# Outgoing products of the first feed-forward block: seven half-size products in place of eight, in three groups

## The chip, the cores and the metric

The kernel runs on one core of one Trainium2 chip. It runs one layer of an encoder on 512 tokens of width 1024, in 32-bit floats. The metric is the time of one execution on the device in microseconds, median of several runs. A core has five engines that work side by side, each through its own queue in order: TensorE (PE in the profile) multiplies, VectorE (DVE) and ScalarE (ACT) do elementwise work, GpSimd (POOL) and SyncE (SP) mostly issue transfers here. Transfers are carried out by 16 DMA engines.

## The reference

The layer has three parts. The first and the third are feed-forward blocks (SwiGLU), the second mixes tokens by two kinds of attention. The change is in the first block:

```python
h = modulate(rmsnorm(x, norm_ffn1[l]), sh1, sc1)
x = x + 0.5 * g1[:, None, :] * swiglu(h, w_ffn1_in[l], w_ffn1_out[l])
# swiglu(h, w_in, w_out): gate, up = split(h @ w_in); (silu(gate) * up) @ w_out
# mod = silu(c) @ w_mod + b_mod gives sh1, sc1, g1 and six more vectors (9 x 1024)
```

x is 512 x 1024, the inner width is 2816. In the kernel everything lies transposed: x is eight tiles (128 rows of the width by 512 tokens), and the inner width is 22 chunks of 128. An outgoing product takes one chunk of activations (128 x 512 tokens) and a 128 x 128 piece of w_ffn1_out, for each of eight output columns m.

## The kernel before

**High and low parts.** [...] To keep precision each operand is split into a high part (an ACT cast, L185) and a low part (a DVE subtraction, L186; `split_from`), and each product is done three times: high by high, high by low, low by high (`mm3`, L174 to L176, for 512 tokens or 256; `two`, L444 to L446, for 256).

**Seven for eight.** A `Unit` multiplies a 2 x 2 matrix of half-size blocks by another with seven products in place of eight (Strassen's way, in Winograd's form). Its seven products are called s1, a11, a12, s2, s3, s4, a22. Three of the weight operands come from HBM by plain loads and the others are made by adding: `ask` loads a block (SP), adds another to it in flight for s1 (`accum_op=ALU.add`, issued by POOL), and `prepare` splits the block into high and low parts and then has POOL add the next block to what lies in the buffer, for the next operand. The result is put together from copies of PSUM banks (ACT, L521) and sums (DVE, L523, L528, L531, after a12, s4 and s3). Operands on the side of the activations are sums as well (`SUMS`): n1, n2, t3, t4 beside b11, b12, b21, b22, of which seven are used.

**First block.** Of the 22 chunks of the inner width the first six are computed by plain products (the first three of them right at the start, beside the norm), and the others in pairs, p = 3 to 10, by eight units of depth 4 (`in_unit1`), at seven for eight. What they leave (`finish`, `in_post1`) is split into high and low parts and kept. The outgoing products are plain (`Out1`): `CHUNKS` has four groups of chunks (0 to 5, 6 to 11, 12 to 15, 16 to 21), and after the units that yield a group's chunks, each of the eight output columns m is multiplied and added to x by DVE (L802, with the gate g1). The last group ends in `boundary`, which does its last `LAST_1` = 4 columns first for tokens 0 to 255 and then for 256 to 511, with the next norm's sums, diagonal and spread at given steps (`TO_MIX`).

**Last block.** It does both its ingoing and its outgoing products by units: after each group of pairs (`PARTS`: 4, 4 and 3) follow two outgoing units, one for each half of the width.

**What sets the order.** `run_items` goes through a list of products. A product's loads are asked for a few products ahead (`ASK`, counted in products of full length) and its weights are split a few ahead (`MAKE`). SP and POOL work strictly in the order in which this list issues; PE, DVE and ACT are put in order by the framework's scheduler. Five places for high and low weight parts (`HILO`) and four for raw weights (`RAW`) are shared. Beside the products the list spends a credit of 0.27 for each (`SIDE`): each full credit lets one of 24 remaining columns of w_mod (512 KB) be loaded by SP and reduced by DVE (`mod_col`, L272). These are needed for g1 (the gate of the outgoing products) and for the next norm.

Of the kernel before, what the change touches and what calls it, by code (L numbers as in the profile page):

```python
# [18 lines left out]
P = 128  # L19
D = 1024  # L20
T = 512
# [87 lines left out]
CHUNKS = (range(0, 6), range(6, 12), range(12, 16), range(16, 22))  # L109
PLAIN, LAST_1 = 3, 4  # L110
# [24 lines left out]
def layer(ctx: ExitStack, tc: tile.TileContext, a: dict):  # L135
# [434 lines left out]

    def sub(out, p, q, negated):

        if negated:
            V.scalar_tensor_tensor(out, p, -1.0, q, ALU.mult, ALU.subtract)
        else:
            V.tensor_tensor(out, p, q, ALU.subtract)
# [26 lines left out]
    cact = [sbuf("ka", [P, D], F32, 1)]  # L603
    hh, hl = new_h()
# [111 lines left out]
    act1 = {}  # L716

    def act_of(p):
        if p not in act1:
            act1[p] = b8()  # L720
        return act1[p]
# [14 lines left out]
    def in_post1(c, v, u):  # L736
# [12 lines left out]
        t, r = act_of(u.p), HALVES[int(c[2]) - 1]  # L749
        split_from(t[:, 0:2, r], t[:, 2:4, r], g.rearrange("p (j q) -> p j q", j=2))  # L750
# [7 lines left out]
    class Out1:  # L758


        def __init__(self, chunks, tag, final):
            self.chunks, self.tag, self.final, self.depth = chunks, tag, final, len(chunks)
            self.length = len(chunks) / 4
            self.ASK, self.MAKE = {m: 3.0 for m in range(NC)}, {m: 1.5 for m in range(NC)}
            self.at, self.ready, self.bank = {}, {}, {}

        def ask(self, m):
            if m not in self.at:
                n, c = self.depth * P, self.chunks.start * P
                t = self.at[m] = sbuf("raw", [P, 1024], F32, RAW)[:, 0:n]  # L770
                nc.sync.dma_start(t, a["w1o"][m][:, c : c + n])

        def by_halves(self, m):
            return self.final and m >= NC - LAST_1

        def prepare(self, m):
            if m not in self.ready:
                self.ask(m)
                aside = FAR if not self.by_halves(m) else STEP_1 if m == NC - LAST_1 else ASIDE
                t = self.ready[m] = high_low(self.depth * P, aside, (self, m))  # L780
# [3 lines left out]
        def products(self, m, po, r, ks):  # L784
            wh, wl = self.ready[m]
            for k in ks:
                q, o = self.chunks[k], slice(k * P, (k + 1) * P)
                t = act_of(q // 2)
                mm3(po, wh[:, o], wl[:, o], t[:, q % 2, r], t[:, 2 + q % 2, r], k == 0, k == self.depth - 1)
                if k == self.depth - 1 and r.stop == T:  # L790
                    let_go((self, m))
                yield

        def multiply(self, m, ks=None):
            if m not in self.bank:
                self.bank[m] = bank(self.tag)
            list(self.products(m, self.bank[m], FULL[0], range(self.depth) if ks is None else ks))

        def after(self, m):
            while any((v, c) == (G1, m) for v, c, *_ in rest + asked):  # L800
                column(rest)
            V.scalar_tensor_tensor(x[m], self.bank[m], modv[G1][:, m : m + 1], x[m], ALU.mult, ALU.add)  # L802
            if self.final:
                n2.add(m)
                spill(m)
# [3 lines left out]
    def item1(u, q, ks=None):  # L809
        items1.append((u, q, ks, side1))  # L810
# [24 lines left out]
    with tc.manual_schedule(engines={mybir.EngineType.SP, mybir.EngineType.Pool}):  # L835
# [4 lines left out]
        for q in range(3, 2 * PLAIN):  # L840
# [12 lines left out]
            finish(q, out)  # L853
            if q == 3:
# [4 lines left out]
        begun = PLAIN  # L859
        for n, chunks in enumerate(CHUNKS):  # L860


            final = n + 1 == len(CHUNKS)
            for p in range(begun, max(chunks.stop // 2, PLAIN + 1)):
                u, nxt = units1[p], units1.get(p + 1)
                if p == PLAIN:
                    item1(u, "s1")
                    item1(u, "a11")
                elif p > begun:
                    item1(units1[p - 1], "a22")  # L870
                if p == PLAIN or p > begun:
                    item1(u, "a12")
                item1(u, "s2")
                if nxt:
                    item1(nxt, "s1")
                item1(u, "s3")
                item1(u, "s4")
# [1059 lines left out]
```

## Time and profile before

| what | before |
|---|---|
| median of 3 runs | 1066.88 us (1066.68 to 1067.96) |
| profiled execution, span | 1066.6 us |
| instructions | 18660 |
| moved by DMA | 220.92 MB |

The profile is of one execution. Its page gives each engine's busy time, then the span in 40 slices (26.7 us each) with a digit for the busy tenths, the DMA queues with the time that their packets took as a share of all 16 engines over the span, and groups of instructions: line, engine, operation, output and inputs, shapes, count, busy time, mean of one in ns, idle time before them and what ended it. A view by windows gives the same sums for given stretches. PE's busy time counts products; PEld counts the weight loads that run beside them. A "share" of DMA is the time that packets took, over 16 engines.

### The profile page before, as it was taken

The page shows a single profiled execution, that of the slowest core. Times are in us where ns is not written, and L with a number is a line of the kernel's source. Part 1 is how long each engine was busy: PE and PEld are TensorE (multiplying, and loading weights), DVE is VectorE, ACT ScalarE, POOL GpSimd, SP SyncE. Part 2 cuts the span into 40 slices and gives each one's busy share as a digit, 9 for nine tenths or more (in the row PEclk, how much of TensorE's full clock was granted, in tenths as well). Part 3 has the DMA queues.
Part 4 walks back from the last instruction along what each step waited for, and adds up shares of the span by engine and source line. Part 5 has one row for each costly group of instructions (what it writes and reads, how often), then busy time and mean ns, then how long its engine had stood idle before and what let it go on. Part 6 is the DMA issues. An engine that isn't in the chain of part 4 may idle for free.

```text
span 1066.6 us, 18660 instructions
## 1 busy us (share of the span) xinstructions
PE 1047.0 (98%) x7316; PEld 953.3 (89%) x7316; DVE 795.7 (75%) x1459; ACT 566.6 (53%) x928; POOL 155.0 (15%) x174
## 2 busy tenths in 40 slices
PE   7999999999999999999999999999999999999998
PEld 5689889899899998888777878989999999999997
DVE  6985666666796679858864578976889777877867
ACT  5564334344354342667676755534766646654553
POOL 1100010100110100443211100001011211112210
PEclk9999999999999999999999999999999999999999
DMA  9968687866975459696356852974498998999974
GB/s 332 362 205 208 207 211 189 264 155 195 281 181 160 164 200 409 215 270 160 99 120 166 239 160 85 351 242 118 101 232 200 215 230 217 220 219 213 219 146 124
DMA packets 69084, 220.92 MB, mean 207 GB/s; under 512 B 8194, under 2 KB 10882, under 8 KB 68995
## 3 DMA queue, kind: packets, MB, share of 16 engines
q1 hardware_dynamic: 46512, 146.52, 38.2%
q0 software_dynamic: 19488, 68.70, 34.9%
q10 hardware_dynamic: 2994, 4.51, 1.2%
q8 instruction: 57, 0.93, 0.3%
q14 instruction: 33, 0.26, 0.1%
HBM read 209.46 MB, written 10.23 MB: 206 GB/s over the span
## 4 chain that ended last, share of the span: by engine, by line
PE 79%; DVE 8%; issue 5%; DMA 3%; ACT 3%; POOL 1%; SPq 0%; ACTq 0%; DVEq 0%; POOLq 0%
PE acc L444 5%; PE acc L446 5%; PE acc L445 5%; PE sc L174 5%; PE sc L175 5%; PE sc L176 5%; PE sc L446 5%; PE sc L444 5%; PE sc L445 5%; PE acc L174 4%; PE acc L176 4%; PE acc L175 4%; PE sc L182 2%; PE acc L1048 2%; PE acc L1049 2%
## 5 line engine op out<-in xcount | busy, mean ns | idle before, releaser
L185 ACT CAST high<-raw 128x1024 fp32r<-128x1024 f32 (+2 forms) x162 | 158.3, 986 | 165.9 <-PE acc L445 38.8
L186 DVE TENSOR_TENSOR low<-raw,high 128x1024 fp32r<-128x1024 f32 (+2 forms) x162 | 183.7, 1141 | 61.2 <-ACT high L185 60.2
L444 PE MATMUL acc<-b,high 128*128 128x256 f32 x508 | 141.0, 278 | 0.3 <-DVE f L523 0.3
L446 PE MATMUL acc<-b,low 128*128 128x256 f32 x508 | 140.6, 277 | 0.2 <-DVE low L186 0.2
L445 PE MATMUL acc<-b,high 128*128 128x256 f32 x508 | 140.6, 277 | 0.1
L444 PE MATMUL sc<-b,high 128*128 128x256 f32 x500 | 138.5, 277 | 1.8 <-ACT f L521 1.8
L446 PE MATMUL sc<-b,low 128*128 128x256 f32 x500 | 138.6, 277 | 1.1 <-DVE low L186 1.1
L445 PE MATMUL sc<-b,high 128*128 128x256 f32 x500 | 138.4, 277 | 0.0
L186 DVE TENSOR_TENSOR low<-u,high 128x1024 fp32r<-128x1024 f32 (+1 forms) x73 | 87.5, 1200 | 28.4 <-ACT high L185 27.1
L185 ACT CAST high<-u 128x1024 fp32r<-128x1024 f32 (+1 forms) x73 | 75.5, 1035 | 56.5 <-PE sc L175 15.9
L174 PE MATMUL sc<-b,high 128*128 128x512 f32 (+1 forms) x280 | 100.8, 360 | 0.0
L175 PE MATMUL sc<-b,high 128*128 128x512 f32 (+1 forms) x280 | 100.4, 359 | 0.0
L176 PE MATMUL sc<-b,low 128*128 128x512 f32 (+1 forms) x280 | 100.2, 358 | 0.0
L444 PEld LDWEIGHTS acc<-b,high 128*128 128x128 f32 x508 | 95.4, 188 | 0.8 <-DVE f L523 0.5
L444 PEld LDWEIGHTS sc<-b,high 128*128 128x128 f32 x500 | 94.0, 188 | 2.2 <-ACT f L521 2.2
L445 PEld LDWEIGHTS acc<-b,high 128*128 128x128 f32 x508 | 95.5, 188 | 0.4 <-DVE b L1725 0.3
L446 PEld LDWEIGHTS acc<-b,low 128*128 128x128 f32 x508 | 95.4, 188 | 0.4 <-DVE low L186 0.4
L446 PEld LDWEIGHTS sc<-b,low 128*128 128x128 f32 x500 | 93.9, 188 | 1.5 <-DVE low L186 1.5
L445 PEld LDWEIGHTS sc<-b,high 128*128 128x128 f32 x500 | 93.9, 188 | 0.0
L174 PE MATMUL acc<-b,high 128*128 128x512 f32 (+1 forms) x248 | 92.7, 374 | 0.0
L176 PE MATMUL acc<-b,low 128*128 128x512 f32 (+1 forms) x248 | 90.0, 363 | 0.0
L175 PE MATMUL acc<-b,high 128*128 128x512 f32 (+1 forms) x248 | 89.8, 362 | 0.0
(369 smaller groups left out, 2676.4 us busy)
## 6 DMA issues: line engine op xcount, KB each, us to landing
u<-w_mod SPq DMA_DIRECT2D x40, 512.0 KB, 7.6
b<-w_mod SPq DMA_DIRECT2D x32, 512.0 KB, 6.0
raw<-w2i SPq DMA_DIRECT2D x31, 512.0 KB, 5.9
u<-w2i POOLq DMA_DIRECT2D x31, 512.0 KB, 6.6
u<-w1u POOLq DMA_DIRECT2D x24, 512.0 KB, 7.1
raw<-w1u SPq DMA_DIRECT2D x24, 512.0 KB, 6.8
raw<-w1o SPq DMA_DIRECT2D x24, 384.0 KB, 4.5
raw<-w_gate SPq DMA_DIRECT2D x16, 512.0 KB, 6.8
```

Source lines behind the costliest of these rows:

```text
L174: PE.matmul(out, wh, xh, start=first, stop=False)
L175: PE.matmul(out, wh, xl, start=False, stop=False)
L176: PE.matmul(out, wl, xh, start=False, stop=last)
L182: PE.matmul(out, of[j][a], of[j][b], start=i == 0, stop=i == 2)
L185: S.copy(hi, src)
L186: V.tensor_tensor(lo, src, f(hi), ALU.subtract)
L444: PE.matmul(out, wh[:, s], xh, start=first and j == 0, stop=False, skip_group_check=True)
L445: PE.matmul(out, wh[:, s], xl, start=False, stop=False, skip_group_check=True)
L446: PE.matmul(out, wl[:, s], xh, start=False, stop=last and j == 1, skip_group_check=True)
L1048: PE.matmul(out[t][:, 0:n], hh[k][:, ht], wh[:, o : o + n], start=k == 0, stop=False)
L1049: PE.matmul(out[t][:, 0:n], hh[k][:, ht], wl[:, o : o + n], start=False, stop=False)
```

## The change

Of the 22 inner chunks, the first 18 (pairs 0 to 8, `PARTS_1`: three groups of three pairs) now go out through units of depth 3: two after each group (`out_unit1`), one for each half of the width. Only the last four chunks (pairs 9 and 10) go out plainly (`Last1`), and `LAST_1` becomes 6, so that six of eight columns are done by halves of the tokens in `boundary`.

For that the activations of pairs 0 to 8 are no longer split whole. `late1` hands each pair to `act_split`, which makes the four differences and splits seven operands of 256 tokens; these come in pieces, one or two beside each product. They are kept in four of the big tiles (`act_tile`), in a new tile `extra` (tag "tabs", whose place the rotary tables take later, in place of `keep` tiles of their own) and in halves of the first block's h that are no longer read (`slot`). The differences of sign that the units need are put into a negated copy of the gate (`minus`). Weights are laid out anew (`w1a`, `w1o`).

```diff
-CHUNKS = (range(0, 6), range(6, 12), range(12, 16), range(16, 22))
-PLAIN, LAST_1 = 3, 4
+PARTS_1 = (range(0, 3), range(3, 6), range(6, 9))
+PLAIN, LAST_1 = 3, 6
...
+    def act_split(b, store):
+        ta, tb = f2(), f2()
+        b.update(n1=ta[:, T1], n2=ta[:, T2], t3=tb[:, T1], t4=tb[:, T2])
+        for o in ("n1", "b11", "b21", "n2", "b22", "t3", "t4"):
+            if o in SUMS:
+                sub(b[o], *(b[q] for q in SUMS[o]), o in NEGATED)
+            hi, lo = store(o)
+            split_from(hi, lo, b[o])
+            yield
...
     def finish(q, out):
-        s, m = f2(), f2()
-        S.activation(s, out[0], AF.Silu)
-        V.tensor_tensor(m, s, out[1], ALU.mult)
-        t = act_of(q // 2)
-        split_from(t[:, q % 2, :], t[:, 2 + q % 2, :], m)
+        values1[q] = m = f2()
+        S.activation(m, out[0], AF.Silu)
+        V.tensor_tensor(m, m, out[1], ALU.mult)
...
+    def out_unit1(part, g):
+        def post(c, v, u):
+            n, t = int(c[1]) - 1, int(c[2]) - 1
+            for j in range(2):
+                m = 4 * g + 2 * n + j
+                xr = x[m][:, HALVES[t]]
+                by = gate_column(m)
+                V.scalar_tensor_tensor(xr, v[:, j * H : (j + 1) * H], by, xr, ALU.mult, ALU.add)
+
+        r = slice(part.start * 2 * P, part.stop * 2 * P)
+        srcs = {q: a["w1a"][g, i][:, r] for i, q in enumerate(("a11", "a12", "a21", "a22"))}
+        u = Unit(srcs, len(part), lambda o, k: act1[o, part.start + k], post, 0)
+        u.p, u.in_order, u.length = None, ("s2", "s4"), len(part) / 4
+        return u
...
+        seq = [units1[PLAIN]]
+        for part in PARTS_1:
+            seq += [units1[p] for p in range(max(part.start, PLAIN) + 1, part.stop + 1) if part.start]
+            seq += [out_unit1(part, g) for g in range(2)]
+        seq += [units1[p] for p in range(PARTS_1[-1].stop + 1, NH)]
...
+        out = Last1()
+        for m in range(2):
+            item1(out, m, ks=range(2), rest=True)
+        for m in range(2):
+            item1(out, m, ks=range(2, out.depth))
+        for m in range(2, NC - LAST_1):
+            item1(out, m)
```

So the order of the first block becomes: unit 3, two out units (pairs 0 to 2), units 4 to 6, two out units (pairs 3 to 5), units 7 to 9, two out units (pairs 6 to 8), unit 10, the plain stage with four chunks.

More of the change, by code (lines that the diff above doesn't have):

```diff
@@ L955, in layer @@
         else:
-            C, R = (keep([P, NT, HD], f"{n}{nm}") for n in "CR")
+            C, R = (four(tabs)[2 * (nm == "kb") + i] for i in range(2))
         g0 = row[:, o : o + NF].unsqueeze(1).broadcast_to([P, NT, NF])
@@ L1813, in late @@
             act_begin()
-        steps = act_split(units[p], p - part.start)
+        u = units[p]
+        b = {f"b{n + 1}{t + 1}": u.v[f"g{t + 1}"][:, r] for t in range(2) for n, r in enumerate(HALVES)}
+        steps = act_split(b, act_store(p - part.start))
         pending.extend([lambda: next(steps)] * 7)
```

212 lines of the change are left out of this document (134 added, 78 removed).

## The prediction

> **What bounds the kernel now.** The page first: busy times, and the slices of the span.
>
> ```profile
> PE 1047.0 (98%) x7316; PEld 953.3 (89%) x7316; DVE 795.7 (75%) x1459; ACT 566.6 (53%) x928; POOL 155.0 (15%) x174
> PE   7999999999999999999999999999999999999998
> DVE  6985666666796679858864578976889777877867
> PEclk9999999999999999999999999999999999999999
> DMA  9968687866975459696356852974498998999974
> q1 hardware_dynamic: 46512, 146.52, 38.2%
> q0 software_dynamic: 19488, 68.70, 34.9%
> ```
>
> PE is busy for 1047.0 of 1066.6 us, at the full granted clock in every slice. So a product removed shortens the run, as long as the others keep up; what they have left decides. The first block's stages came next. These are its inner units and plain outgoing stages in turn: unit 3, out, units 4 and 5, out, units 6 and 7, out, units 8 to 10. Columns: length, then busy time of PE, PEld, DVE, ACT and POOL, granted clock, DMA share, GB/s.
>
> ```profile
> 89.96:117.39 27.43, 27.43 (x241) 27.42 (x240) 19.52 (x27) 13.98 (x20) 0.86 (x1) 1.00 0.60 169
> 117.39:150.06 32.67, 32.67 (x147) 27.03 (x145) 20.15 (x28) 7.97 (x9) 3.46 (x4) 1.00 0.80 225
> 150.06:190.52 40.46, 38.68 (x338) 38.48 (x336) 28.63 (x38) 20.31 (x27) 3.45 (x4) 1.00 0.75 208
> 190.52:223.18 32.66, 32.66 (x146) 27.03 (x145) 17.99 (x26) 7.97 (x9) 3.48 (x4) 1.00 0.91 269
> 223.18:262.85 39.67, 38.91 (x338) 38.53 (x336) 28.72 (x37) 20.30 (x28) 3.45 (x4) 1.00 0.57 146
> 262.85:284.63 21.78, 21.78 (x98) 18.02 (x97) 16.18 (x22) 7.26 (x10) 2.59 (x3) 1.00 1.00 291
> 284.63:334.16 49.53, 49.53 (x434) 49.33 (x432) 41.04 (x72) 26.83 (x37) 5.80 (x7) 1.00 0.74 194
> ```
>
> From 89.96 to 334.16 us, 244.2 us, PE idles 2.5 us (1.78 in the third row, 0.76 in the fifth). DVE's busy times add up to 172.2 us (0.71 of the stretch). The DMA shares times the lengths give 183.7 us (0.75). Both have room, most of it in the plain outgoing stages, where DVE is busy for 0.55 to 0.74 of the time. Those stages are what the change takes away.
>
> The last block already does its outgoing products in the new way. Three windows of it:
>
> ```profile
> 780.00:825.00 45.00, 45.00 (x397) 45.00 (x396) 39.76 (x65) 30.26 (x49) 7.82 (x9) 1.00 0.93 213
> 853.00:900.00 47.00, 47.00 (x414) 47.00 (x414) 36.04 (x52) 24.34 (x34) 7.87 (x10) 1.00 0.96 236
> 970.00:1000.00 30.00, 30.00 (x266) 30.00 (x265) 22.95 (x36) 13.74 (x21) 4.88 (x6) 1.00 0.95 227
> ```
>
> There PE does not idle with DVE at 0.77 to 0.88 and the DMA engines at 0.93 to 0.96. But that block has no w_mod columns beside it; the first block has 24.
>
> **The change, part by part.**
>
> *PE.* Removed: 18 chunks x 8 columns of output x 3 = 432 products 512 wide. An outgoing stage is 6 x 8 x 3 = 144 of them in 32.67 us: 0.2269 us each, 98.0 us. Added: 6 out units x 7 x 18 = 756 products 256 wide. The 853 window has 414 of these in 47.00 us: 0.1135 us each, 85.8 us. PE gains 12.2 us. The last four chunks stay plain: six columns by halves with four chunks are 24 steps of 0.34 us, as four columns with six chunks were, so the passage to the mixers keeps its length and I cost it at nothing. What hides the norm's chain there is the nine steps between its sums (step 4) and its spread (step 13), 3.1 us; without that cover PE would wait about as long.
>
> [...]
>
> *DVE.* Rows of the first and last block (count, busy us, mean ns of one), and two neighbours of the timeline:
>
> ```profile
> L186 DVE TENSOR_TENSOR low<-raw,high 128x768 fp32r<-128x768 f32 x24 | 22.6, 952 | 10.2 <-ACT high L185 10.2
> L186 DVE TENSOR_TENSOR low<-u,high 128x1024 fp32r<-128x1024 f32 x21 | 25.7, 1223 | 5.3 <-ACT high L185 4.8
> L802 DVE SCALAR_TENSOR_TENSOR x<-sc,mod,x 128x512 f32<-128x512 f32 x24 | 18.0, 749 | 22.7 <-PE sc L176 22.6
> L186 DVE TENSOR_TENSOR b<-f,b 128x512 fp32r<-128x512 f32 x17 | 11.7, 687 | 4.0 <-ACT b L185 4.0
> L272 DVE CUSTOM_DVE_ANT_0 b<-b,ka,par 128x1024 f32<-128x1024 f32 x8 | 10.2, 1278 | 0.0
> L186 DVE TENSOR_TENSOR b<-f,b 128x256 fp32r<-128x256 f32 x69 | 26.9, 419 | 2.1 <-ACT b L185 1.8
> L1651 DVE SCALAR_TENSOR_TENSOR x<-f,mod,x 128x256 f32<-128x256 f32 x28 | 12.3, 482 | 0.5
> L528 DVE TENSOR_TENSOR f<-f,op 128x512 f32<-128x512 f32 x8 | 5.5, 682 | 1.2 <-PE op L446 1.2
> ...
> 367.05 0.48 DVE L346 SCALAR_TENSOR_TENSOR f<-x,mod,tp 128x256 f32<-128x256 f32 x1
> 367.44 0.48 DVE L351 SCALAR_TENSOR_TENSOR b<-f,mod,b 128x256 fp32r<-128x256 f32 x1
> ```
>
> The two neighbours start 0.39 apart though each lasts 0.48, so I take 0.085 off each row. Counts are those of the two kernels' instructions. Added: 63 low parts of activations 256 wide (0.334: 21.0 us), 36 differences of the same size (12.1), 18 low parts of weights 768 wide (0.867: 15.6), 52 updates of x 256 wide (0.397: 20.6), 18 sums of products (0.597: 10.7), some small ones (0.5). Removed: 18 low parts 512 wide (0.602: 10.8) and 26 updates of x 512 wide (0.664: 17.3). Net 52.4 us. Of this the splits of pairs 0 and 1 (22 x 0.334 less 5 x 0.602, 4.3 us) fall before 90 us; 48.1 us come after. DVE then has 172.2 + 48.1 = 220.3 us to do in the 244.2 - 12.2 = 232.0 us that PE needs: 0.95, against 0.88 in the fullest window quoted of the last block.
>
> It is not even. In the changed order of DVE, between the sum after s3 of the first out unit of the second group and the same sum of the second, stand 3 weights 1024 wide (1.138), 5 of 768, 3 columns (1.193 and some 0.15 of small ones each), 8 updates of x, 3 sums and 2 low parts of activations: 17.3 us, for 7 x 18 x 0.1135 = 14.3 us of PE. Counted likewise the first group has 16.6 and the third 16.3, and the stretches around them are below PE's time. The excess is 2.3 + 3.0 + 2.0 = 7.3 us. If the lead of the prepared weights covers it, the loss is 0; if none of it is covered, 7.3 us.
>
> *DMA.* The loads of outgoing weights by SP stay 24 of 384 KB (the plain ones shrink from 8 x 384 to 8 x 256 KB), and SP and POOL get them in another order. New are 24 accumulating transfers of 384 KB from POOL. The queue q0, nearly all accumulating, took 34.9% of 1066.6 us for 68.70 MB, 5.42 us of all 16 engines per MB; q1 took 38.2% for 146.52 MB, 2.78. So 9.44 MB x 5.42 = 51.1 us are added and 1.05 MB x 2.78 = 2.9 us go: 183.7 + 48.2 = 231.9 us, for 232.0 us of PE. That is a share of 1.00. The highest share over 40 us beside a PE without idle time is 0.96 (853 window); 1.00 stood for 21.8 us (262.85 window). At 0.96 the stretch would last 241.6 us, 9.6 more than PE. So the loss is between 0 (the queues run at 1.00 with enough lead) and 9.6 us.
>
> [...]
>
> *ACT, POOL and what waits for what.*
>
> ```profile
> L185 ACT CAST b<-f 128x256 fp32r<-128x256 f32 x69 | 25.3, 404 | 10.9 <-DVE f L1602 6.9 <-DVE f L576 2.8 <-DVE f L574 0.9
> L185 ACT CAST high<-raw 128x768 fp32r<-128x768 f32 x24 | 19.6, 836 | 19.3 <-PE sc L175 7.5 <-DMA raw<-w1o 7.1 <-PE sc L176 1.9
> L185 ACT CAST b<-f 128x512 fp32r<-128x512 f32 x17 | 10.6, 621 | 16.0 <-DVE f L748 16.0
> L521 ACT COPY f<-acc 128x512 f32<-128x512 f32 x12 | 7.0, 584 | 2.6 <-PE acc L446 2.6
> ...
> POOL raw L499 <- DVE low L186: 73.0, 6, 17.5
> DVE low L186 <- ACT high L185: 34.1, 26, 3.9
> PE sc L444 <- ACT f L521: 1.8, 1, 1.8
> PE sc L446 <- DVE low L186: 0.8, 1, 0.8
> ```
>
> ACT gets 63 x 0.404 + 18 x 0.836 + 18 x 0.584 - 18 x 0.621 = 39.8 us on 104.6: 0.62 of 232 us, hidden behind PE; if PE were quicker still, DVE would stop it first. POOL issues 24 more transfers, some 0.79 us each (7.87 us for 10 in the 853 window), 19 us on 21.0 of 232: hidden. But its queue is in order: the waits (total, times, longest) show POOL standing 73.0 us behind DVE's low parts, since an accumulating load may only follow the split of what lies in its buffer. A late DVE makes POOL's next transfer late, everything behind it in that queue too, and with it DVE's next split. So the two loads at their limit feed on each other. On the other side a wait for one gives the other time: the two losses lie on the same stretch and don't simply add.
>
> PE's two waits of today, 2.5 us, sit in the inner units behind the first two outgoing stages; I let them go into the new idle time. That new idle time is between 0 and 7.3 + 9.6 = 16.9 us. No row is near enough to choose one end: the stretch lies as far above the last block's windows (DVE 0.95 to 0.77-0.88, DMA 1.00 to 0.93-0.96, none of which lost anything) as the bounds reach. I take the middle, 8.5 us.
>
> *Sum.* Against the profiled execution (1066.6 us span, 0.3 us under the 1066.88 us median, which is what I take for the rest around it): 1066.9 - 12.2 - 2.5 + 8.5 = 1060.7, say 1060.
>
> **The rivals.**
> - *All of it arrives.* The lead covers the excess, and PE stays gapless as in the last block: 1066.9 - 14.7 = 1052.2, with 1 us of idle time 1053. For it: DVE's slices show a 9 (0.9 or more) at 293 to 320 us without loss, and DMA held 1.00 for 21.8 us. Against: here it must hold for 200 us, with columns. Chance 0.18.
> - *DMA and DVE become the bound together.* The accumulating transfers run behind from the second out unit on, POOL's queue hands the delay to DVE's splits and these to PE, none of both losses is covered and today's 2.5 us stay: 1066.9 - 12.2 + 16.9 = 1071.6, slower. It decides from 14.7 us of idle time in the stretch on (6% of 232 us). For it: the share of 1.00, and that half the room DVE had was in the plain stages. Against: no window without loss shows that either limit has been reached. Chance 0.28.
> - *No change.* The idle time eats the gain to within 2.1 us. Chance 0.09.
> - *Half-wide products cost more than half* (weight loads that no longer hide): each 10 ns above 113.5 costs 756 x 0.01 = 7.6 us, so at 130 ns the run is at 1066.9 - 12.2 + 12.5 = 1067.2 and beyond that slower. 414 of them in 47.00 us are evidence enough against it; under 0.01, within the slower case.
>
> **How the numbers follow.** The forecast (idle time 3 to 12.5 us, 1055 to 1064.7) has 0.45. Faster by over 0.2% (2.1 us, about what these runs can tell from none; they spread by 1.3 us) are it and the first rival, 0.63; the same 0.09; slower 0.28. For 8 times in 10 the range goes from the first rival's 1052 to 1073, a little over the second's 1071.6, as a delay in POOL's queue has no upper bound in these rows.
>
> **What would show it.** Right: 324 more products (756 - 432), still 0.227 and 0.1135 us apart; between unit 3 and the plain stage DVE is at 0.9 or more and the DMA share near 1; PE's new waits name DVE's low parts, ACT's copies or w1a and w1u transfers, mostly in or just after the out groups, until the columns end; and the end of unit 10 comes within some 5 us of where it was, the rest of the gain in the plain stage, 10.9 us shorter. Wrong: PE idle under 2 us (lead enough) or over 14 us (bound moved), or a loss behind the first block, which I cost at nothing.

## The result and the profile after

The changed kernel takes 1086.45 us (median of 4 runs, 1085.53 to 1088.18) against 1066.78 us for the kernel before on the same chip: 1.0186 times as long, 95% interval 1.0174 to 1.0198. The forecast was 1060 us, within 1052 to 1073; the result lies above that range: the change makes the kernel slower, not faster.

The page of the changed kernel: its busy times, slices and queues.

```profile
PE 1047.7 (97%) x7640; PEld 968.3 (89%) x7640; DVE 845.6 (78%) x1608; ACT 600.1 (55%) x1011; POOL 175.7 (16%) x198
PE   7999998899899999999999999999999999999997
DVE  6988878789887778876875468877789777877877
PEclk9999999999999999999999999999999999999999
DMA  9967997899976529797455861876398998899974
q0 software_dynamic: 22944, 78.13, 39.0%
q1 hardware_dynamic: 46512, 146.52, 37.3%
```

PE's busy time did not fall (1047.0 before), although 12.2 us of products went: some of what is left ran slower. The slices show 8s from 163 to 217 us and from 271 to 298 us, in the inner units that follow the first two groups of out units. To find the place, the run is cut in two windows, units (first product of unit 3 to the last of unit 10) and passage (plain stage by halves up to the value projection); columns as in the prediction's windows. First the kernel before, then the changed one:

```profile
89.96:334.16 244.20, 241.67 (x1730) 225.85 (x1728) 172.22 (x245) 104.62 (x139) 23.10 (x27) 1.00 0.75 209
334.16:387.73 53.57, 53.23 (x382) 49.82 (x380) 38.54 (x77) 26.55 (x45) 5.82 (x10) 1.00 0.40 131
```

```profile
90.27:357.72 267.45, 249.91 (x2101) 246.94 (x2100) 221.37 (x382) 138.24 (x215) 44.96 (x52) 0.97 0.87 228
357.72:406.21 48.49, 46.16 (x335) 43.95 (x333) 37.05 (x80) 24.96 (x45) 5.86 (x10) 0.93 0.40 138
```

By count of products the stage by units should be 1.3 us shorter than before (242.9 with before's 2.5 us of idle time kept) and the passage 10.9 us shorter (42.7). They are 24.5 and 5.8 us over that. From the value projection on (387.73 us before, 406.21 after) both kernels take the same time to 0.3 us. So the loss of 30.3 us less the 12.2 us saved, 18.1 us, is nearly all of the 18.7 us between the spans (1066.6 and 1085.3).

The predicted loads were right: VectorE (DVE) is busy 221.4 us in the stage (220.3 forecast), and a DMA share of 0.87 over 267.45 us is 232.7 us (231.9 forecast). What they cost was wrong. PE's waits in the stage by units, longest groups (total, times, longest):

```profile
PE acc L444 <- ACT f L521: 7.3, 4, 3.8
PE acc L444 <- DVE f L523: 4.1, 1, 4.1
PE sc L444 <- ACT f L521: 3.2, 2, 3.0
PE op L446 <- DVE low L186: 1.6, 1, 1.6
```

PE waits little for weights themselves (low parts, L186: 2.6 us in all); it waits for copies of its own banks (L521) and a sum behind one (L523). One of these waits, followed back through the timelines of SP, POOL, ACT, DVE and PE:

```profile
145.41 0.44 SPq L478 DMA_DIRECT2D u<-w1u  x1
...
155.16 0.86 POOL L480 DMA_DIRECT2D u<-w1u  x1 [11.20 <-DMA u<-w1u]
...
164.24 1.04 ACT L185 CAST high<-u 128x1024 fp32r<-128x1024 f32 x1 [7.94 <-DMA u<-w1u]
...
165.32 1.23 DVE L186 TENSOR_TENSOR low<-u,high 128x1024 fp32r<-128x1024 f32 x1 [7.43 <-ACT high L185]
...
168.20 0.58 PE L444 MATMUL acc<-b,high 128*128 128x256 f32 x1 [4.05 <-DVE f L523]
```

An inner unit's block u was asked for at 145.41 us. POOL could issue the addition to it only at 155.16, after waiting 11.20 us for the load. ScalarE (ACT) stood 7.94 us at the split of that block, DVE 7.43 us behind ACT, and the copy and the sum that PE needed stood behind them in order. PE lost 4.05 us. The same three stretches, load, addition and split with what follows it, by windows:

```profile
145.41:155.16 9.75, 8.42 (x70) 8.18 (x70) 9.43 (x19) 4.96 (x8) 0.00 (x0) 1.00 1.02 341
155.16:164.24 9.08, 8.75 (x72) 8.55 (x72) 2.54 (x3) 1.14 (x2) 1.75 (x2) 1.00 1.00 268
164.24:168.20 3.96, 0.00 (x0) 0.00 (x0) 2.88 (x6) 3.40 (x6) 0.00 (x0) 0.99 0.23 46
```

While the load and the addition were on their way, the DMA engines were full (shares 1.02 and 1.00; the sum of packet times can come out a little over 1); while PE waited, they were nearly idle (0.23). The 0.87 of the whole stage is a mean of such stretches.

Then a cost that is in no term of the prediction. The clock record of the changed kernel is at 0.5 for 3.413 us each from 168.09, 198.81, 297.80, 349.00, 376.31 and 389.96 us; the kernel before has none from 17.9 to 1065.8 us. PE right behind the wait followed above:

```profile
169.65 0.41 PE L444 MATMUL acc<-b,high 128*128 128x256 f32 x1
169.86 0.41 PE L445 MATMUL acc<-b,high 128*128 128x256 f32 x1
170.08 0.41 PE L446 MATMUL acc<-b,low 128*128 128x256 f32 x1
```

The products are 0.2135 us apart instead of 0.1133: 16 in place of 30 in 3.413 us, 1.6 us lost each time, 9.6 us in six. Four of the six lie in the stage by units (6.4 us), two in the passage (3.2 us). Ten gaps in the stage are over 0.4 us longer than the usual 0.11 us between starts of products; together they are 18.9 us, and 25.3 with the 6.4. The kernel before has 2.9 us of such gaps, which the 242.9 us contain, so 22.4 of the 24.5 us found above are accounted for; the rest is in smaller gaps.

### The profile page after: what moved, and what is told of

Its sections match the earlier page's. It is cut to its first block, busy times and chain, and to the rows that moved or that the text cites. A ratio compares the mean times of both kernels' runs of the same rounds, so it can differ in the third digit from the quotient of the medians.

```text
span 1085.3 us, 19611 instructions
## 1 busy us (share of the span) xinstructions
PE 1047.7 (97%) x7640; PEld 968.3 (89%) x7640; DVE 845.6 (78%) x1608; ACT 600.1 (55%) x1011; POOL 175.7 (16%) x198
## 4 chain that ended last, share of the span: by engine, by line
PE 52%; DVE 5%; issue 5%; ACT 2%; DMA 2%; POOL 1%; DVEq 0%; POOLq 0%; ACTq 0%
PE acc L444 4%; PE acc L445 4%; PE acc L446 4%; PE acc L174 3%; PE acc L176 3%; PE acc L175 3%; PE sc L444 3%; PE sc L445 3%; PE sc L446 3%; PE acc L1169 2%; PE sc L182 2%; PE acc L1170 2%; PE acc L1171 2%; PE tp L1247 1%; PE sc L174 1%
## 5 line engine op out<-in xcount | busy, mean ns | idle before, releaser
L185 ACT CAST high<-raw 128x1024 fp32r<-128x1024 f32 (+2 forms) x162 | 158.6, 986 | 124.5 <-PE acc L445 18.9
L186 DVE TENSOR_TENSOR low<-raw,high 128x1024 fp32r<-128x1024 f32 (+2 forms) x162 | 183.7, 1141 | 41.0 <-ACT high L185 40.5
L444 PE MATMUL acc<-b,high 128*128 128x256 f32 x606 | 170.9, 282 | 11.7 <-ACT f L521 7.3
L446 PE MATMUL acc<-b,low 128*128 128x256 f32 x606 | 169.8, 280 | 0.4 <-DVE low L186 0.4
L445 PE MATMUL acc<-b,high 128*128 128x256 f32 x606 | 169.8, 280 | 0.1
L444 PE MATMUL sc<-b,high 128*128 128x256 f32 x598 | 166.5, 278 | 3.2 <-ACT f L521 3.2
L446 PE MATMUL sc<-b,low 128*128 128x256 f32 x598 | 166.3, 278 | 0.6 <-DVE low L186 0.6
L445 PE MATMUL sc<-b,high 128*128 128x256 f32 x598 | 166.1, 278 | 0.0
L186 DVE TENSOR_TENSOR low<-u,high 128x1024 fp32r<-128x1024 f32 (+1 forms) x91 | 104.7, 1151 | 51.8 <-ACT high L185 48.3
L185 ACT CAST high<-u 128x1024 fp32r<-128x1024 f32 (+1 forms) x91 | 90.5, 997 | 88.4 <-DMA u<-w1a 21.0
L444 PEld LDWEIGHTS acc<-b,high 128*128 128x128 f32 x606 | 116.1, 192 | 13.2 <-ACT f L521 8.4
L446 PEld LDWEIGHTS acc<-b,low 128*128 128x128 f32 x606 | 115.9, 191 | 1.0 <-DVE low L186 1.0
L444 PEld LDWEIGHTS sc<-b,high 128*128 128x128 f32 x598 | 113.2, 189 | 3.8 <-ACT f L521 3.8
L445 PEld LDWEIGHTS acc<-b,high 128*128 128x128 f32 x606 | 116.0, 191 | 0.3 <-DVE b L1841 0.3
L445 PEld LDWEIGHTS sc<-b,high 128*128 128x128 f32 x598 | 113.1, 189 | 0.0
L185 ACT CAST b<-f 128x256 fp32r<-128x256 f32 (+1 forms) x132 | 49.6, 411 | 27.4 <-DVE f L815 7.4
L186 DVE TENSOR_TENSOR b<-f,b 128x256 fp32r<-128x256 f32 (+1 forms) x132 | 52.7, 426 | 8.2 <-ACT b L185 7.8
L174 PE MATMUL sc<-b,high 128*128 128x512 f32 (+1 forms) x160 | 55.0, 343 | 0.0
```

What stands on the lines that cost most here:

```text
L174: PE.matmul(out, wh, xh, start=first, stop=False)
L185: S.copy(hi, src)
L186: V.tensor_tensor(lo, src, f(hi), ALU.subtract)
L444: PE.matmul(out, wh[:, s], xh, start=first and j == 0, stop=False, skip_group_check=True)
L445: PE.matmul(out, wh[:, s], xl, start=False, stop=False, skip_group_check=True)
L446: PE.matmul(out, wl[:, s], xh, start=False, stop=last and j == 1, skip_group_check=True)
```

## The experiments

The theories here: (1) transfers come late, since the DMA engines and the queue of additions are overloaded; (2) VectorE is too full; (3) an idle stretch of PE is followed by half clock, and so costs more than itself; and, for the passage, that it has a price of its own. Units and passage are windows as above, unless the text says otherwise; an expectation may count the stage by units to the start of its last product, 0.1 us less.

### Less work for the DMA engines, less for VectorE

*Columns not loaded:*

```
-            asked.append((v, c, mod_load(v, c, w)))
+            if columns is rest and len(columns) < 22:
+                nc.sync.dma_start(w[:, 0:64], a["w_mod"][v * NC + c][:, 0:64])
+                asked.append((v, c, w))
```

> The changed kernel, with 22 of the 24 loads of modulation columns in the first block cut to 64 of their 1024 entries (the columns are then not those of the reference). It takes 22 x 0.49 MB x 2.78 us = about 30 us off the DMA engines between 57 and 350 us, 22 places of 512 KB off SP's queue, and leaves VectorE's work as it is. If the DMA engines are what holds the first block up (theory 1), most of the idle time of TensorE there goes: 1086 - 15 to 22 = 1064 to 1071 us. If VectorE is (theory 2), it stays at 1083 to 1087.

*Columns not reduced:*

```
-            out=w, in0=w, in1=cact[0], scale=by, ...
+            out=w[:, 0:k], in0=w[:, 0:k], in1=cact[0][:, 0:k], scale=by, ...     # k = 64 for G1, SC2, SH2
```

> The changed kernel, with the 24 reductions of columns on VectorE cut from 1024 to 64 entries (the columns are then not those of the reference); all loads stay. It takes 24 x about 1.1 = 26 us off VectorE between 57 and 350 us and nothing off the DMA engines. Theory 2 (VectorE holds the block up): 1064 to 1071 us. Theory 1 (the DMA engines): 1083 to 1087 us; a little less if loads are issued earlier because VectorE sets buffers free earlier.

*Out units without their adding transfers:*

```
-                G.dma_start(t, self.srcs[src], accum_op=ALU.add)
+                if self.add:                       # False for out units; the same in ask()
+                    G.dma_start(t, self.srcs[src], accum_op=ALU.add)
```

> The changed kernel with the 24 adding transfers of the new out units left out (their summed weights are then only one of the quarters). VectorE, ScalarE and TensorE do the same work; the DMA engines lose 24 x 384 KB at 5.42 us per MB = about 48 to 51 us, and a weight block that waited for load and addition waits for the load alone. Theory 1: nearly all of the 23 us lost between 57 and 350 us comes back, with the half-clock stretches that stand behind idle time there: 1062 to 1068 us. Theory 2: no more than 4 us comes back, 1082 to 1087.

*Columns not loaded and out units without additions:*

> The changed kernel with both loads cut: the 22 columns' loads to 64 of 1024 entries and the adding transfers of the out units left out, so that some 80 us of the DMA engines' work are gone between 57 and 350 us; VectorE's work is as in the changed kernel. Each alone brought 9 and 12 us. If the DMA engines are the whole cause of the waits in the stage by sevens, they add up until only the passage is left: 1066 to 1070 us. If a rest of waits comes from the order in which VectorE and ScalarE work (copies and splits in one queue), it ends at 1071 to 1075, and waits for copies on ScalarE remain with the DMA share under 0.8.

*No additions in any of these units, columns not loaded:* as above, with `u.add = False` for every unit of the sequence.

> The changed kernel with 54 adding transfers of the first block left out, those of the out units (24 of 384 KB) and of the inner units (30 of 512 KB), and 22 columns' loads cut to 64 of 1024 entries. VectorE, ScalarE and TensorE do the same work as in the changed kernel. So far the stage by units (267.3 us, 242.8 by the count of products) gave back 7.6 us for about 30 us of transfers, 14.0 for 51, and 18.1 for both. If all that is lost there is lost to weights that come late, it now falls to 243 to 245 us, and the kernel to 1062 to 1065 us with the passage as it is (48.6). If VectorE or the order of the queues holds a rest, 247 to 250 us remain, and the kernel at 1067 to 1070.

| kernel | us | units | passage | DMA share x length in units |
|---|---|---|---|---|
| before | 1066.78 | 244.2 | 53.6 | 183 |
| changed | 1086.45 | 267.5 | 48.5 | 233 |
| columns not reduced | 1084.55 | 267.3 | 48.3 | 233 |
| columns not loaded | 1077.18 | 259.8 | 48.7 | 213 |
| out units not added | 1074.59 | 253.4 | 49.2 | 188 |
| both not loaded/added | 1069.80 | 249.4 | 49.4 | 167 |
| no additions, columns not loaded | 1063.06 | 242.5 | 49.5 | 85 |

All but the first two rows leave out parts of the weights or of the sums, so they tell of the time alone. The stage by units of the one without reductions and of the last two:

```profile
90.29:357.63 267.34, 251.93 (x2101) 249.20 (x2100) 200.80 (x382) 139.12 (x214) 44.97 (x52) 0.97 0.87 228
```

```profile
88.63:338.02 249.39, 244.40 (x2101) 242.44 (x2100) 221.22 (x382) 139.02 (x214) 24.88 (x29) 0.99 0.67 166
```

```profile
88.41:330.92 242.51, 242.18 (x2102) 240.81 (x2100) 220.90 (x382) 140.35 (x214) 0.57 (x1) 1.00 0.35 110
```

The first row takes 20.6 us off DVE and the stage stays as long: VectorE is not the cause. The last row has DVE as full as ever, 220.9 of 242.51 us (0.91), and PE loses 0.3 us: theory 2 falls, and late transfers are shown as the cause of the loss in this stage. That row also says what the arithmetic saves when nothing comes late: 1063.06 us is 0.9958 of the kernel before (0.9944 to 0.9972), with the slower passage still in it (49.5 us: it is not late transfers that make the passage slow).

Transfers taken away give time back step by step, whichever they are: about 20 us of transfers 7.6, about 45 us 14, about 66 us 18, about 148 us 25. Two things speak against the engines' total over the stage as the only measure. With the additions of the out units gone the engines have as much to do as in the kernel before (188 and 183 us) and the stage is still 10.5 us over the 242.9; and the shares of the two rows above the last one, 0.74 and 0.67, are below those at which the last block ran without a wait. But these are means again: in the 10 us that end with the longest wait of PE in the run without the out units' additions (2.68 us, until 154.96) the share is 1.02. So the prices I had expected ("most of the idle time goes" for the columns, "nearly all" for the out units' additions) were too high for either alone.

### When weights are asked for, and when they are split

*Blocks s1 asked for 12 places ahead, not 9:*

```
+            u.ASK = {"s1": 12, "a11": 7, "a12": 5, "a22": 6}
```

> The changed kernel, with the first weight block of each unit of the first block (the one that is loaded and then added to, s1) asked for 12 places ahead rather than 9; the others as they were. If the waits come from the time that a load and its addition take in queues that are full (theory 1), three places more (some 6 to 8 us) cover the waits for u blocks: 5 to 10 us back, 1076 to 1081 us. If the engines' total is the limit, earlier requests only displace others: 1084 to 1088.

*Columns spread thinner:*

```
-EARLY, NEXT, SIDE, LATER = 3, 3, 0.27, 4
+EARLY, NEXT, SIDE, LATER = 3, 3, 0.2, 4
```

> The changed kernel, with the modulation columns of the first block spread thinner: 0.20 of a column per place rather than 0.27 (the first eight are still forced by the first out units). Same loads and reductions in all, fewer of them while units 5 to 8 and the second out units run. Theory 1 and theory 2 both expect a gain from a smoother load, 2 to 6 us: 1080 to 1084; if the waits lie where the first columns are forced, nothing: 1085 to 1088.

*Splits later, behind the last copy* (with the moved passage and the ring turned so that the mixers begin at the same place as before, both below):

```
+            u.MAKE, u.in_order = {"s1": 3, "a11": 2, "a12": 2, "s2": 2, "s4": 2, "s3": 2, "a22": 2}, u.MAKE
```

> The changed kernel with two edits: the splits of weight blocks of the units of the first block are made 3 or 2 places ahead (not 5 to 2) and behind the last copy of a bank in ScalarE's order, and the passage has the places of the earlier run. Loads, additions and arithmetic are the same. If TensorE's waits come from copies of its banks that stand in ScalarE's queue behind a split whose transfer is late, copies overtake splits, and most of the 3 to 5 us waits for copies go: 1083.3 - 5 to 12 = 1071 to 1078 us. If the DMA engines' total alone decides, weights come late whoever waits for them: 1081 to 1085 us, with waits for the low parts in place of waits for copies.

Measured: 1088.43 us (units 266.2) for the earlier requests, at the upper end of the second reading. 1090.92 us (units 271.4) for the thinner columns, a miss for every reading. It says nothing about the columns, as this row of DVE shows:

```profile
120.86 0.17 DVE L1027 CAST posf<-pos 128x4 f32<-128x4 int32 x1 [7.84 <-DMA pos<-pos]
```

The load of the positions goes out when fewer than 20 columns are left, so it came later with them, and DVE, in order, stood 7.84 us at their conversion; PE then waited 7.5 us for a low part. 1107.68 us (units 288.1) for the later splits, a clear miss: a split that comes later also frees its buffer and starts its addition later. Its waits of PE name ScalarE's split (high, L185) where they named copies: the copies did stand behind the splits, but with the copies in front PE waited for the late weights themselves.

### Sevens for fewer chunks

Groups of three, three and two pairs with six plain chunks behind; then one group of two pairs (chunks 12 to 15), the others plain as in the kernel before:

```
-PARTS_1 = (range(0, 3), range(3, 6), range(6, 9))
-PLAIN, LAST_1 = 3, 6
+PARTS_1 = (range(0, 3), range(3, 6), range(6, 8))
+SEVENS = (True, True, True)          # one group: (False, False, True)
+PLAIN, LAST_1 = 3, 4
```

> The changed kernel with sevens on 16 of the 22 chunks (groups of three, three and two pairs) and the last six plain, so that the passage to the mixers is the one of the kernel before again (last four output tiles by halves, six chunks each). TensorE has 1.36 us more work than with 18 chunks. If the passage with four chunks costs 6 to 7 us by itself, it comes back: 1086.5 + 1.4 - 6.5, and some 2 for eight smaller adding transfers: 1078 to 1083 us, the passage within 1 us of the kernel before, and the waits between 150 and 300 us as in the changed kernel. If the passage was late only because of the groups by sevens, it stays at 1086 to 1089.

> Sevens for one group alone, chunks 12 to 16 (two pairs), behind two plain groups and in front of six plain chunks. TensorE saves 96 products 512 wide and makes 168 of 256: 21.8 - 19.0 = 2.7 us; eight adding transfers of 256 KB are added, some 11 us of the DMA engines, at a place where most modulation columns have been loaded. If sevens pay where the DMA engines have room, 1064 to 1066 us, 1 to 3 under the kernel before; if the waits come with any group by sevens (one 3 to 4 us wait with its half clock each), 1068 to 1073.

Sixteen chunks took 1090.82 us: units 260.1, passage 53.8, which is the passage of the kernel before again, as the first reading had it. But its mixers took 354.9 us where the kernel before and the changed one take 349.2 and 349.0, and the total missed. One group took 1087.38 us (1083.76 to 1091.12), over both readings: units 257.5, passage 53.6, mixers 359.5. What sets these kernels apart is the place in the ring of five weight buffers (`turn` in `high_low`) at which the mixers begin: 4 in the kernels before and after, 0 with sixteen chunks, 1 with one group. Two runs with the ring turned back to 4 (the first with the later splits, the second with s1 asked for 12 places ahead and all columns loaded ahead of the group):

```
+        turn[0] += (0 - turn[0]) % HILO          # ahead of the last output tiles
```

> One group by sevens (chunks 12 to 16) with the later splits, and with the ring of five weight buffers turned so that the passage and the mixers find the places of the kernel before (the run with one group entered the mixers at another place of the ring, and its mixers took 359.5 us against 349.2). Ring: mixers at 349 us again, 10 us back. Queue theory: the stage by units, 257 us in that run, falls to 242 to 246: 1087.4 - 10.3 - 11 to 15 = 1062 to 1066 us. If the waits stay: 1074 to 1078 us.

> One group by sevens (chunks 12 to 16), the ring turned to the place of the kernel before, columns at 0.45 of one per place (all loaded before the group by sevens begins), and s1 blocks asked for 12 places ahead; splits as in the changed kernel. The earlier run of one group had 257.3 us in the stage by units (241.4 by the count of products); the ring gives 10 us back in the mixers: 1077 without more. If columns in the group's stretch and late requests make half of the waits there: 1068 to 1073 us. If the demand of inner and out units back to back (four loads and four additions each) is enough by itself: 1075 to 1079.

1086.33 and 1086.27 us. The mixers are back at 349.3 and 349.8 us, so the place in the ring is what made them longer (the last section says where they lose it); but the stage by units took 261.5 and 260.6 us. Both expectations missed: by count of products that stage is 241.5 us, and in the three runs one group by sevens alone loses 16 to 20 us there. In the last run the last column is asked for at 239.5 us, ahead of the group, and the DMA share around it is 0.72:

```profile
262.00:300.00 38.00, 32.44 (x239) 31.34 (x238) 22.42 (x39) 16.88 (x30) 8.79 (x10) 0.87 0.72 154
```

On the mean there is room on the engines, and weights are late all the same. POOL and ACT in that stretch:

```profile
292.83 0.86 POOL L481 DMA_DIRECT2D u<-w1u  x1 [8.23 <-DMA u<-w1u]
293.37 1.22 POOL L500 DMA_DIRECT2D u<-w1u  x1
294.35 1.12 POOL L500 DMA_DIRECT2D raw<-w1a  x1
294.93 1.43 POOL L500 DMA_DIRECT2D u<-w1a  x1
```

```profile
304.92 0.62 ACT L186 CAST high<-raw 128x512 fp32r<-128x512 f32 x1 [7.36 <-DMA raw<-w1a]
```

POOL stood 8.23 us at the addition for an inner unit whose load had not landed (SP had asked for that load only at 288.56), with three more additions behind it. Then all four went out within 2.1 us, and the split of the third got its block at 304.92, 10.6 us after its issue. The DMA engines in these two stretches:

```profile
284.60:292.83 8.23, 7.90 (x66) 7.49 (x64) 6.82 (x12) 5.08 (x9) 0.00 (x1) 1.00 0.73 156
294.35:304.92 10.57, 7.88 (x68) 7.68 (x66) 3.81 (x8) 3.21 (x7) 2.87 (x4) 1.00 1.06 218
```

They had room while POOL stood, and were full once everything went out together; PE's longest wait, 6.06 us, ended at 308.29. So I read theory 1 in a sharper form: each summed block is a chain (buffer free, load, addition, split, low part, next addition) through POOL's one queue in order, and the work comes in bunches that fill the engines. The plain outgoing stages may have been the time in which that queue caught up, and sevens add four additions per out unit just there. This is a reading of the traces. No run changes the order of the queue alone, or the speed of the engines alone, so which of the two sets the price is not shown.

### The passage to the mixers

*The kernel before with the passage of the changed one:* groups of 6, 6, 6 and 4 chunks, six tiles by halves; the second time with the ring turned back.

```
-CHUNKS = (range(0, 6), range(6, 12), range(12, 16), range(16, 22))
-PLAIN, LAST_1 = 3, 4
+CHUNKS = (range(0, 6), range(6, 12), range(12, 18), range(18, 22))
+PLAIN, LAST_1 = 3, 6
```

> The kernel before, with its groups of plain chunks cut as 6, 6, 6 and 4 rather than 6, 6, 4 and 6, and the last six (rather than four) output tiles computed by halves: the passage to the mixers as the changed kernel has it, without products by sevens. In the changed kernel this stretch (350 to 406 us) lost 6.9 us to uneven starts of products where the kernel before lost 1.05. If that loss belongs to the passage itself, 1066.8 + 4 to 7 = 1071 to 1074 us, with stretches of half clock behind the two sums of halves; if it was only passed on from the stage by sevens, 1066 to 1068 us.

> The kernel before with groups of 6, 6, 6 and 4 chunks and six output tiles by halves, as in the earlier run, but with the ring of weight buffers turned so that the mixers find it as in the kernel before. If the place in the ring is what made the mixers 5.7 us longer there (354.8 against 349.2 us), 1082.1 - 5.7 = 1076 to 1077 us, mixers 349 us, and what is left over 1067.3, some 9 us, is the passage's own price. If not: 1081 to 1083.

*The passage's places moved, in the changed kernel:*

```
-TO_MIX = (4, 13, 2, 2, 4, 2, 1)
+TO_MIX = (6, 14, 4, 2, 2, 4, 1)
```

> The changed kernel with the places in the passage moved: first sum behind step 6 rather than 4, its spread at 14 rather than 13, two more steps of gate products ahead of the second sum, and two fewer steps of hidden values of the first half ahead of the last updates of x. Nothing is added or removed. If the passage loses time because updates of x, squares and additions by halves take about 1.3 us per output tile one behind the other, while the four-chunk products of one tile take 1.36 us, and the hidden values stand in front of the last of them on VectorE, then later sums find them done: both waits (0.73 and 1.35 us) and the half clock behind them go, 1086 - 4 to 6 = 1080 to 1082 us. If the loss there has another cause: 1085 to 1088.

*Spare products ahead of the sums:*

```
+                for _ in range(self.fill):          # 4 x 3 products
+                    mm3(self.st[r.start][:, 0 : 2 * P], *self.by, True, True)
```

> The changed kernel, with twelve spare products 256 wide (12 x 0.1133 = 1.36 us) put on TensorE in front of each of the two sums of squares of the passage to the mixers, into the bank that the sum then starts afresh. TensorE was idle there 0.73 and 1.35 us. Theory 3 (each idle stretch is followed by 3.4 us of half clock, some 1.6 us lost): the half-clock records at 376 and 390 us go, and the kernel is 1.6 to 3.2 us faster less at most 0.6 us for the products: 1083 to 1085 us. If the half clock has nothing to do with the idle time before it, the records stay, and the time is 1086 to 1087.

The new passage in the old kernel took 1082.06 us, more than any reading; 5.7 us of it were the ring (mixers 354.8 us). With the ring turned: 1076.93 us, mixers 349.9. So the regrouping with its passage costs the kernel before some 10 us (ratio 1.0098, 1.0080 to 1.0115) without any product by sevens: its passage takes 53.1 us where the count of products gives 42.7, with three stretches of half clock (granted clock 0.90 on the mean of the passage). In the changed kernel the same passage is 5.8 us over. The second sum of squares of the changed kernel, and its cause on DVE:

```profile
387.74 0.61 PE L337 MATMUL op<-ones,f 128*128 128x2 f32 x4 [1.19 <-DVE f L295]
```

```profile
384.94 0.48 DVE L369 SCALAR_TENSOR_TENSOR x<-sc,mod,x 128x256 f32<-128x256 f32 x1
385.90 0.43 DVE L295 TENSOR_TENSOR f<-f,f 128x256 f32<-128x256 f32 x1 [0.48 <-ACT f L289]
386.24 0.48 DVE L369 SCALAR_TENSOR_TENSOR x<-sc,mod,x 128x256 f32<-128x256 f32 x1
387.26 0.43 DVE L295 TENSOR_TENSOR f<-f,f 128x256 f32<-128x256 f32 x1 [0.54 <-ACT f L289]
```

Update, square and addition of one tile follow those of the tile before, 1.36 us per tile, and DVE only reaches the last ones after the hidden values of the first half. With six chunks a tile has 18 products of 0.1133, 2.04 us, and the chain stays ahead; with four it has 12, 1.36 us, and the chain ends last. With the places moved the passage takes 45.9 us instead of 48.5, no half clock falls in it, and the kernel 1083.29 us (1081.89 to 1084.33; 1080 to 1082 was expected):

```profile
358.60:404.48 45.88, 43.88 (x339) 41.81 (x338) 36.60 (x80) 25.52 (x45) 5.86 (x10) 1.00 0.41 140
```

The spare products gave nothing (1089.05 us, over both readings; passage 48.4): the record at 376 us went, but PE still waited 1.1 us for the same addition ahead of the second sum, with half clock behind it. Why the wait did not shrink by the 1.36 us of products put there stays open.

### Idle time and the clock

*Idle time put into the kernel before,* first in a plain group, then in the passage (there with a gate weight in place of `wh`):

```
+                    for i in range(LOOPS):          # 4, then 8
+                        PE.matmul(spare, wh[:, 0:P], loop, start=True, stop=True)
+                        S.copy(loop, spare)
```

> The kernel before, with one artificial idle stretch on TensorE: ahead of output tile 4 of its second group of plain chunks, four times one small product and a copy of its result by ScalarE, each waiting for the other, 3 to 5 us in all. Theory 3 (an idle stretch of that length is followed by half clock): a record of 0.5 for 3.4 us behind it, with products 512 wide twice as far apart, and the kernel slower by the idle time and 1.6 us more. If idle time alone is the price, the clock stays at 1.0 and the kernel is slower by the idle time.

> The kernel before, with an idle stretch of TensorE that can't be filled: in the passage, where the order of TensorE, VectorE and ScalarE is written out by hand, behind the first half-wide output tile, eight times a small product and a copy of its result by ScalarE, each waiting for the other, 4 to 8 us in all. Theory 3: one or two records of half clock for 3.4 us each behind it, and the kernel slower by the idle time and 1.6 us for each. If idle time alone is the price, the clock stays at 1.0.

The first told nothing: the scheduler put other products between, PE idled some 0.5 us, the clock stayed at 1.0 and the time at 1067.21 us. In the second, the order is fixed. From 353.79 to 361.19 us PE did nothing but eight small products. The clock record is at 0.5 from 358.34 to 365.17 us, and the kernel took 1076.64 us:

```profile
360.96 0.38 PE L398 MATMUL op<-loop,u 128*128 128x16 f32 x1 [0.26 <-ACT loop L399]
361.19 0.56 PE L174 MATMUL sc<-b,high 128*128 128x256 f32 x1
361.55 0.42 PE L175 MATMUL sc<-b,high 128*128 128x256 f32 x1
361.77 0.41 PE L176 MATMUL sc<-b,low 128*128 128x256 f32 x1
```

The passage is 9.4 us longer (62.97 against 53.57): 7.4 us of idle time, and 18 products at 0.2135 in place of 0.1133 us, 1.8 us. A second record, at 177.4, stands behind a wait of 2.4 us in an inner unit of that run. Theory 3 holds in a kernel with no other change, though not for every wait: the kernel before waits 1.94 us at 174.7 and has no record behind it.

## Why the prediction was wrong, step by step

- *PE, 12.2 us of products:* right to some 2 us. With nothing late the stage by units takes 242.5 us (244.2 less 2.5 of idle time and 1.3 of products would be 240.4), and the products stand 0.2269 and 0.1133 us apart at full clock. The rival that half-wide products cost more than half is out.
- *The two loads:* right to some 1 us (221.4 and 232.7 us), and wrong as a measure of what they cost. The step "DVE ... the loss is 0 ... 7.3 us" had the wrong engine: no run shows a loss in this stage from DVE's load. The step "the loss is between 0 ... and 9.6 us" for the DMA engines was the one that failed most. It turned the load of the engines, averaged over the whole stage, into a delay. What the runs show instead: late transfers cost PE the stage's 24.5 us, half clock included, since leaving out the additions and the columns' loads gives 24.9 us back with DVE as busy as before. The transfers come in bunches: in the wait followed above the engines are full for 18.8 us and nearly idle behind that, and one group by sevens without columns beside it, at a mean share of 0.72, still loses some 19 us. The windows of the last block at 0.96 without a wait were no bound for that. How much of the delay is the order of POOL's queue and how much the full engines stays open.
- *"Two loads at their limit feed on each other":* the way was right (late addition, ACT's split, DVE, PE), the second load was not needed for it: 20.6 us less of it changed nothing. PE is idle for 17.5 us in the stage (267.45 less 249.91), over the upper end of 16.9, and I had taken the middle, 8.5.
- *The granted clock:* the sum has no term for it. It cost 6.4 us in the stage and 3.2 in the passage. The six records are 3.413 us long each, and their starts are 9, 29, 15, 8 and 4 times that apart. Records stand behind waits of only 0.7 and 1.35 us around the sums of the passage, while a wait of 1.94 us in the kernel before, at 174.7, was not followed by a record.
- *The passage, "costed at nothing":* wrong by 5.8 us. The cover named (nine steps between sum and spread) was there; what failed lies ahead of it, in front of the sums: the chain of update, square and addition per tile had 2.04 us of products to hide behind and got 1.36.
- *The rivals:* the second (slower) came nearest with 1071.6 us and named POOL's queue; it lacked the clock, the passage and most of the delay, and it blamed DVE as well.
- *What would show it wrong:* two of the named signs came, PE idle over 14 us and a loss behind the first block's units.

Of the versions by sevens that compute the whole, none beats the kernel before; the fastest is the changed kernel with the passage moved, 1083.29 us.

## What to carry to other kernels

A busy share near 1 is not a price; follow one block from its request to its use, count the transfers and queues that it passes one behind the other, and ask what work gave that chain time to catch up before you remove that work. Where tiles get shorter, compare the products of one tile with the chain of small operations per tile that ran beside them. And when a change makes TensorE wait, look for half clock behind the wait: in the changed kernel it stood behind waits of 0.7 to 4.05 us, not behind every wait, and cost some 1.6 us each time.

## What the runs showed of the hardware that was not expected

- The six records of half clock in the changed kernel are 3.413 us long and stand behind idle time of PE. In the last run with one group by sevens three come in a row, with a granted clock of 0.87 on the mean of 262 to 300 us. The length of the wait alone does not decide in these traces: in the changed kernel PE is idle for 0.8 to 3.4 us of the 3.413 us ahead of a record, while idle times of 1.55 us there (from 144.70) and 1.78 us in the kernel before (from 174.98) had none behind them.
- The same instructions in the mixers take 349, 354.8 or 359.5 us, depending on which of five weight buffers comes first (place 4, 0 or 1). PE is busy 346.6 us in the first case and 352.1 in both others. The granted clock has a part in it: with place 0 in the kernel before, all of the 5.7 us is lost between 533 and 553 us, at a wait of 1.34 us for a split and a record of half clock from 536.00 to 542.83 right behind it; with place 1 waits of 1.36 and 3.02 us are followed by one from 550.13 to 556.96; with place 4 the wait there is 0.8 us, and the granted clock is 1.00 over the mixers of the kernels before and after (0.99 with places 0 and 1). Why the place makes the wait longer was not tried.

```profile
535.18 0.50 PE L174 MATMUL acc<-b,high 128*128 128x512 f32 x1 [1.34 <-ACT high L991]
```
